# Seven block products in place of eight in the second layer's gated feed-forward of a two-layer hybrid backbone

## The chip, the cores and the metric

One NeuronCore of one Trainium2 chip runs the whole program. The metric is the device time of one execution in microseconds. The profile is of one execution; its span runs from the first instruction to the last.

## What is computed

Two layers, each a mixing sub-layer (three groups of heads) and a gated feed-forward. There are 512 latent and 256 context tokens; in layer 1's feed-forward only the 512 latent ones are left. The part that matters here:

```python
def rms_norm(x, g):
    xf = x.astype(F32)
    y = xf * lax.rsqrt(jnp.mean(xf * xf, axis=-1, keepdims=True) + EPS)
    return (y * g.astype(F32)).astype(x.dtype)

def conv_ffn(h, P):
    gt = dwconv(h @ P["w_gate"], P["ffn_conv_w"], P["ffn_conv_b"])
    return (jax.nn.silu(gt) * (h @ P["w_val"])) @ P["w_down"]
...
        h2 = modulate(rms_norm(x_lat, norm2_g[l]), sh2, sc2)
        x_lat = x_lat + g2 * conv_ffn(h2, P)
```

Here h is 512 x 1024, w_gate and w_val are 1024 x 2816, w_down is 2816 x 1024, and the convolution runs over three neighbouring tokens. All is float32.

## The kernel before

Activations lie transposed in SBUF, features on the 128 partitions and tokens along the free dimension: xT and the normed input have 8 blocks k of 128 features. Each float32 operand is split in a rounded part and a rest of a shorter format (hi and lo), and each product is made of three matmuls, hi x hi, hi x lo and lo x hi (mm3, L315 to L317). Weights are loaded as raw (L252, one DMA of 512 KB on SP's queue, three buffers), cast to whi by ScalarE (L260), and VectorE makes wlo = raw - whi (sub_lo, L108). The weight is the stationary operand, the tokens are the moving one.

The feed-forward runs over 22 tiles j of 128 hidden features, in two halves of 11. In a tile, TensorE makes the gate's and the value's product (pp, 8 blocks k each, 512 columns in layer 1); ScalarE makes the first tap with the bias (L1061), VectorE the two others (L1062, L1064), ScalarE the Silu (L99), VectorE the product with the value (L1069), and ft is split into gh (ScalarE, L1070) and gl (VectorE). After 11 tiles the down projection (pd, four pairs of 128 output features) adds into xT (L1100); the gate and value tiles have eight PSUM banks, shared with pd.

The input of layer 1's feed-forward is made by Norm.apply: for each k and each 256 tokens VectorE makes nt (L351), ScalarE hhi (L355) and VectorE hlo (L356); nt has three buffers. The first tile's matmuls follow k by k, and then ScalarE loads the table for Silu.

While layer 0's feed-forward runs, VectorE also makes layer 1's modulation by dot products (L232, in the first half) and splits layer 1's input weights ahead (split_ahead, L283 to L297: loads araw, writes both parts to DRAM). A scheduler orders the instructions on each engine by priorities; each engine then works strictly in that order. SP's queue issues all DMAs in order.

Of the kernel before, what the change touches and what calls it, by code (L numbers as in the profile page):

```python
# [16 lines left out]
P = 128  # L17
# [44 lines left out]
N1H, N1P = 5, 2  # L62

# [7 lines left out]
LPOS = (5, 2)  # L71

# [6 lines left out]
def tile_backbone(  # L79
# [27 lines left out]
    def sub_lo(o, a, hi, eng=None):  # L107
        (eng or V).tensor_sub(o, a, hi.bitcast(F32))  # L108
# [193 lines left out]

    def wsplit_of(key, src, shape, eng, tags=("hi", "lo"), p=None, **kw):
# [19 lines left out]
    class Norm:  # L323
        def __init__(self, np_, nb=2):
            self.p, self.nb = np_, nb
            self.ss = np_.tile([P, TOK], F32, tag="nss", name="nss", bufs=1)
            self.rs = np_.tile([P, TOK], F32, tag="nrs", name="nrs", bufs=1)
            self.begun = set()
# [19 lines left out]
        def apply(self, l, n, g, k, hhi, hlo):  # L348
# [5 lines left out]
            sh = modv[:, l, s, 3 * n, k:k + 1]  # L354
            r = S.activation(hhi[:, k, a:b], t[:, :b - a], AF.Identity, bias=sh)  # L355
# [16 lines left out]
    for l in range(DEPTH):  # L372
# [398 lines left out]
        yp = pool(ystack, f"y{l}", side)  # L771
# [182 lines left out]
        kvs.close()  # L954
# [9 lines left out]
        norm = Norm(np_)  # L964
        table(T_LNEXP)
        with ExitStack() as ph:
# [27 lines left out]
            for k in range(KD):  # L994
                norm.apply(l, 1, g0, k, hhi, hlo)
        if not last:
            ystack.close()
            layer.close()


        with ExitStack() as ph:
            hp = pool(ph, f"g_{l}", "right")
            sp = pool(ph, f"s4_{l}", "right")
# [12 lines left out]

            if not last:
                dots = ExitStack()
                dp = pool(dots, "dots", "left")
            HJ = NJ // 2  # L1020

            if not last:
                norm = Norm(np_)
            for half in range(2):
                gh = hp.tile([P, HJ, toks], F32R, tag="gh", name="gh", bufs=1)
                gl = hp.tile([P, HJ, toks], F32R, tag="gl", name="gl", bufs=1)
                for jj in range(HJ):
                    j = half * HJ + jj
                    pp = [[ps.tile([P, 512], F32, tag="acc", name="pp", bufs=8) for g in range(2)]
                          for s in range(nseg)]  # L1030
                    w = [wsplit(w_gv[l, j, g], [KD, P], "dve") for g in range(2)]

                    def gv(g, seg):
                        a, b, s = seg
                        o = pp[s][g][:, a - SEG[s][0]:b - SEG[s][0]]
                        for k in range(KD):
                            mm3(o, w[g][0][:, k], w[g][1][:, k], hhi[:, k, a:b], hlo[:, k, a:b], k == 0, k == KD - 1)

                    if j == 0:
# [16 lines left out]
                    t = sp.tile([P, TOK], F32, tag="ft", name="ft", bufs=FTB)
                    for s in range(nseg):
                        a, b = SEG[s]
                        gp = pp[s][0]
                        n = b - a  # L1060
                        S.activation(t[:, a:b], gp[:, :n], AF.Identity, bias=fb[:, l, j:j + 1], scale=fw[:, l, j, 1:2])  # L1061
                        V.scalar_tensor_tensor(out=t[:, a + 1:b], in0=gp[:, 0:n - 1], scalar=fw[:, l, j, 0:1],  # L1062
                                               in1=t[:, a + 1:b], op0=ALU.mult, op1=ALU.add)
                        V.scalar_tensor_tensor(out=t[:, a:b - 1], in0=gp[:, 1:n], scalar=fw[:, l, j, 2:3],  # L1064
                                               in1=t[:, a:b - 1], op0=ALU.mult, op1=ALU.add)
                    act(t[:, :toks], t[:, :toks], AF.Silu)
                    for s in range(nseg):
                        a, b = SEG[s]
                        V.tensor_mul(t[:, a:b], t[:, a:b], pp[s][1][:, :b - a])  # L1069
# [137 lines left out]
```

## Time and profile before

| | |
|---|---|
| median of 3 runs | 1595.66 us (1593.68 to 1596.8) |
| profiled execution | 1593.64 us |
| its span | 1591.9 us |
| TensorE busy | 1555.6 us, 98% of the span |
| VectorE busy | 1015.4 us, 64% |
| ScalarE busy | 643.0 us, 40% |
| GpSimd busy | 108.0 us, 7% |
| mean granted TensorE clock | 0.995 of full speed |
| layer 0, feed-forward | about 403 to 960 us |
| layer 1, feed-forward | about 1215 to 1588 us |

The shares are means over stages with different limits. The rows below give them by stage, then single instructions of the places that the change touches. A busy time of TensorE is modelled at its end, so starts are compared.

### The profile page before, as it was taken

Reading aid. Unit: us, or ns where it says so; the run is one execution under the profiler, and the core shown is the slowest. Engines: PE = TensorE matmul, PEld = TensorE weight load, DVE = VectorE, ACT = ScalarE, POOL = GpSimd, SP = SyncE. Lnnn points to the kernel's source line nnn. Section 1 sums busy time; section 2 is a strip of 40 time slices with the busy share of each in tenths; the row PEclk is TensorE's granted clock in tenths of the full one; section 3 lists DMA queues with packets and bytes.
Section 4 is the critical chain, followed back from the end, with each engine's and each line's share of the span. In section 5 each row is a group of like instructions: output and inputs, shape, how many; then the busy total and the mean of one; then the engine's idle time right before and its main releaser. Section 6 shows DMA issues by size and latency. Waiting matters only on the chain.

```text
span 1591.9 us, 21110 instructions
## 1 busy us (share of the span) xinstructions
PE 1555.6 (98%) x8186; PEld 1287.7 (81%) x8186; DVE 1015.4 (64%) x1713; ACT 643.0 (40%) x1115; POOL 108.0 (7%) x128
## 2 busy tenths in 40 slices
PE   6999998999999999999999999999999999999999
PEld 4767786778888888888888887877778888888888
DVE  4489879969999972244454454996977444334433
ACT  5423668853522221133333333265765333133321
POOL 1102134310000000000000000002410000000000
PEclk8999999999999999999999999999999999999999
DMA  8652110014355872126666486542011222322232
GB/s 286 240 187 63 54 54 14 14 67 172 106 185 190 291 246 63 64 68 220 196 199 210 147 278 220 195 153 81 14 54 57 99 97 86 99 94 93 93 110 89
DMA packets 76372, 208.77 MB, mean 131 GB/s; under 512 B 11504, under 2 KB 13808, under 8 KB 76144
## 3 DMA queue, kind: packets, MB, share of 16 engines
q1 hardware_dynamic: 76272, 207.43, 39.5%
q8 instruction: 64, 1.05, 0.3%
q14 instruction: 36, 0.29, 0.1%
HBM read 183.28 MB, written 24.12 MB: 130 GB/s over the span
## 4 chain that ended last, share of the span: by engine, by line
PE 75%; DVE 2%; ACT 1%; issue 0%; POOLq 0%; DVEq 0%; ACTq 0%
PE pp L316 13%; PE pp L315 13%; PE pp L317 13%; PE pd L315 6%; PE pd L317 6%; PE pd L316 6%; PE acc L483 2%; PE acc L484 2%; PE acc L491 2%; PE wo L315 2%; PE wo L316 2%; PE wo L317 2%; PE po L902 1%; PE accC L540 0%; PE accC L538 0%; PE accC L539 0%
## 5 line engine op out<-in xcount | busy, mean ns | idle before, releaser
L260 ACT CAST whi<-raw 128x1024 fp32r<-128x1024 f32 (+1 forms) x174 | 178.2, 1026 | 521.0 <-PE pp L316 247.8
L316 PE MATMUL pp<-hlo,whi 128*128 128x512 f32 (+1 forms) x1072 | 380.6, 356 | 0.8 <-DVE hlo L356 0.8
L315 PE MATMUL pp<-hhi,whi 128*128 128x512 f32 (+1 forms) x1072 | 379.9, 356 | 1.5 <-ACT whi L260 1.3
L317 PE MATMUL pp<-hhi,wlo 128*128 128x512 f32 (+1 forms) x1072 | 378.9, 354 | 0.0
L108 DVE TENSOR_TENSOR wlo<-raw,whi 128x1024 fp32r<-128x1024 f32 (+2 forms) x159 | 189.4, 1194 | 284.4 <-ACT whi L260 279.5
L315 PEld LDWEIGHTS pp<-hhi,whi 128*128 128x128 f32 x1072 | 201.4, 188 | 35.2 <-ACT whi L260 2.7
L316 PEld LDWEIGHTS pp<-hlo,whi 128*128 128x128 f32 x1072 | 201.5, 188 | 32.7 <-DVE hlo L356 1.5
L317 PEld LDWEIGHTS pp<-hhi,wlo 128*128 128x128 f32 x1072 | 201.5, 188 | 31.3
L315 PE MATMUL pd<-gh,whi 128*128 128x512 f32 (+1 forms) x550 | 192.9, 351 | 0.0
L316 PE MATMUL pd<-gl,whi 128*128 128x512 f32 (+1 forms) x550 | 192.3, 350 | 0.0
L317 PE MATMUL pd<-gh,wlo 128*128 128x512 f32 (+1 forms) x550 | 192.3, 350 | 0.0
L317 PEld LDWEIGHTS pd<-gh,wlo 128*128 128x128 f32 x550 | 103.4, 188 | 15.2
L316 PEld LDWEIGHTS pd<-gl,whi 128*128 128x128 f32 x550 | 103.5, 188 | 15.0
L315 PEld LDWEIGHTS pd<-gh,whi 128*128 128x128 f32 x550 | 103.4, 188 | 15.1
L733 DVE SCALAR_TENSOR_TENSOR cacc<-cin,cw,cacc 128x783 f32<-128x783 f32 (+1 forms) x120 | 105.0, 927 | 3.4 <-ACT cacc L728 3.4
L1069 DVE TENSOR_TENSOR ft<-ft,pp 128x256 f32<-128x256 f32 (+1 forms) x66 | 39.4, 598 | 96.2 <-PE pp L317 84.8
L232 DVE CUSTOM_DVE_ANT_0 mraw<-mraw,csil,bmod 128x1024 f32<-128x1024 f32 x64 | 81.6, 1278 | 7.5 <-DMA mraw<-in_w_modT_dram 7.3
L483 PE MATMUL acc<-whi,hhi 128*128 128x512 f32 x192 | 78.5, 409 | 0.0
L99 ACT ACTIVATE ft<-ft 128x768 f32<-128x768 f32 (+1 forms) x44 | 32.5, 740 | 113.0 <-DVE ft L1064 112.9
L484 PE MATMUL acc<-whi,hlo 128*128 128x512 f32 x192 | 76.6, 399 | 0.0
L99 ACT ACTIVATE e<-pss,mx 128x768 f32<-128x768 f32 (+1 forms) x80 | 65.1, 816 | 16.3 <-DVE mx L857 14.8
L857 DVE TENSOR_REDUCE mx<-pss 128x1 f32<-128x768 f32 (+1 forms) x80 | 67.2, 845 | 4.1 <-PE pss L855 3.1
(220 smaller groups left out, 2498.3 us busy)
## 6 DMA issues: line engine op xcount, KB each, us to landing
raw<-in_w_gv_dram SPq DMA_DIRECT2D x88, 512.0 KB, 3.3
mraw<-in_w_modT_dram SPq DMA_DIRECT2D x64, 512.0 KB, 4.2
raw<-in_w_down_dram SPq DMA_DIRECT2D x34, 512.0 KB, 3.6
wh<-in SPq DMA_DIRECT2D x24, 512.0 KB, 4.4
wl<-in SPq DMA_DIRECT2D x24, 512.0 KB, 4.3
raw<-in_w_in_dram SPq DMA_DIRECT2D x20, 512.0 KB, 3.7
araw<-in_w_in_dram SPq DMA_DIRECT2D x40, 256.0 KB, 3.4
in<-ahi SPq DMA_DIRECT2D x40, 256.0 KB, 4.6
```

The lines of the kernel that those rows point to most:

```text
L99: r = S.activation(out, in_, func, **kw)
L108: (eng or V).tensor_sub(o, a, hi.bitcast(F32))
L232: r = V.tensor_tensor_reduce(out=junk, in0=w, in1=csil[:, s], scale=1.0, scalar=bmod[:, l, i, f:f + 1], op0=ALU.mult, op1=ALU.add, accum_o ...
L260: S.copy(hi, raw)
L315: T.matmul(o, lhi, rhi, start=start, stop=False)
L316: T.matmul(o, lhi, rlo, start=False, stop=False)
L317: T.matmul(o, llo, rhi, start=False, stop=stop)
L483: T.matmul(pt[t], hhi[hs], wh[:, a], start=k2 + a == 0, stop=False)
L484: T.matmul(pt[t], hlo[hs], wh[:, a], start=False, stop=False)
L733: V.scalar_tensor_tensor(out=cacc[:, c, :cn], in0=cin[:, c, j:j + cn], scalar=cw[:, l, c, j:j + 1], in1=cacc[:, c, :cn], op0=ALU.mult, op1 ...
L857: V.tensor_reduce(out=mx, in_=pss[:, :nk * P], op=ALU.max, axis=AX.X, negate=True)
L1069: V.tensor_mul(t[:, a:b], t[:, a:b], pp[s][1][:, :b - a])
```

## The change

In layer 1's feed-forward, tiles 4 to 21 make gate and value together with seven block products in place of eight. The tokens are taken in blocks of 128: even blocks and odd blocks are the two columns of a 2 x 2 block product, the lower and the upper four k are its inner halves, gate and value are its rows. The eight products of a plain tile have each 4 blocks k and 256 columns; the seven need sums of the operands. Sums of the weights are made by sum_quarters (four VectorE operations of 512 columns a tile). For 14 tiles it runs in layer 0 (sum_ahead: two loads pgv, the sums, two writes to DRAM, all DMAs on SP's queue); for tiles 8, 9, 16 and 17 it runs in layer 1. Sums of the tokens are made once: GpSimd writes the full normed input hf from nt (a new instruction in Norm.apply), half_forms makes four sums, three of them split again in hi and lo, and third_form puts the fourth over the odd blocks of the lower half of hhi and hlo after the last plain tile.

A seven tile loads four weights (a1, two sums, a22: 1.75 MB). Its products go into three PSUM banks, al, de and be, in the order 1, 7 of the tile before, 5, 2, 4 of the tile before, 6, 3; al is read out after products 1 and 6 while later products add onto it. Read-outs go to gs and vs in SBUF by three ScalarE copies (L1232, L1234, L1238) and three VectorE sums (L1236, L1240, L1242); the product with the value is two operations of 256 columns (L1248, L1249). The tiles go in groups of 8, 8 and 6, with a down projection after each; layer 0 keeps 11 and 11 and plain tiles. Other edits free and take pools in another order.

```diff
+GROUPS = ((11, 11), (8, 8, 6))
+SEVEN = (False, True)
+NPLAIN = 4
...
+SUMJ = (0, 2, 4, 6, 8, 10)
+MSUM, ESUM = ((1, 2, 3), (0,)), ((0, 1, 2, 3), (0,))
+AHEAD = (4, 5, 6, 7, 10, 11, 12, 13, 14, 15, 18, 19, 20, 21)
...
+    def sum_quarters(gr, vr):
+
+        lo_, hi_ = slice(0, KD // 2), slice(KD // 2, KD)
+        r = V.tensor_add(vr[:, hi_], vr[:, lo_], vr[:, hi_])
+        V.tensor_sub(vr[:, lo_], gr[:, lo_], vr[:, lo_])
+        V.tensor_sub(gr[:, lo_], vr[:, hi_], gr[:, lo_])
+        V.tensor_sub(gr[:, hi_], gr[:, hi_], gr[:, lo_])
+        return r
+
+    def sum_ahead(sp):
...
+            if ready:
+                x, w = ready
+                summed[x] = dram.tile([P, 2, KD, P], F32, name=f"gv_{x}")
+                r = sum_quarters(*w)
+                tc.add_manual_dep(r.ins, after.name, NOSYNC, reason="data of the step before")
+                for g in range(2):
+                    nc.sync.dma_start(out=summed[x][:, g], in_=w[g])
+            if j is not None:
+                w = [sp.tile([P, KD, P], F32, tag=t, name="pgv", bufs=2) for t in ("hi", "lo")]
+                for g in range(2):
+                    nc.sync.dma_start(out=w[g], in_=w_gv[1, j, g])
...
-        def apply(self, l, n, g, k, hhi, hlo):
+        def apply(self, l, n, g, k, hhi, hlo, full=None):
...
+            if full is not None:
+                G.tensor_scalar(out=full[:, k, a:b], in0=t[:, :b - a], scalar1=sh, scalar2=None, op0=ALU.add)
...
+        def half_forms(g):
...
+            V.tensor_sub(t1, q12, q11)
+            V.tensor_sub(t2, q22, t1)
+            V.tensor_sub(t3, q22, q12)
+            V.tensor_sub(t4, q21, t2)
+            for x, (fh, fl) in ((1, f1), (2, f2), (4, f4)):
+                S.copy(fh[:, :, a // 2:b // 2], tt[x])
+                sub_lo(fl[:, :, a // 2:b // 2], tt[x], fh[:, :, a // 2:b // 2])
+
+        def third_form():
+
+            for g, t3 in t3s.items():
...
+                o = od(hhi, slice(0, KD // 2), a, b)
+                S.copy(o, t3)
+                sub_lo(od(hlo, slice(0, KD // 2), a, b), t3, o)
...
+            def seven_weights(j):
+                a1 = wload(w_gv[l, j, 0], [KD, P])
+                ws = {}
+                for g, p in ((1, wp), (0, rg)):
+                    ws[g] = p.tile([P, KD, P], F32, tag="raw", name="raw", bufs=RAWB if p is wp else 2)
+                    nc.sync.dma_start(out=ws[g], in_=summed[j][:, g] if j in summed else w_gv[l, j, g])
+                a22 = rg.tile([P, KH2, P], F32, tag="a22", name="a22", bufs=2)
+                nc.sync.dma_start(out=a22, in_=w_gv[l, j, 1, :, KH2:])
...
+                return {1: (a1, 0), 2: (a1, 1), 7: (sv, 0), 5: (sv, 1), 6: (sg, 0), 3: (sg, 1), 4: ((h2, l2), None)}
...
+                    prod(j, i, {1: al, 6: al, 7: al, 4: al, 5: de, 3: de, 2: be}[i], i in (1, 5, 2))
+                    with tc.high_priority(offset=EVP):
+                        if i == 1:
+                            S.copy(evt(gs), blk(al))
+                        elif i == 5:
+                            S.copy(vs, de)
+                        elif i == 2:
+                            V.tensor_add(evt(gs), blk(be), evt(gs))
+                        elif i == 6:
+                            S.copy(odt(gs), blk(al))
+                        elif i == 3:
+                            V.tensor_add(odt(gs), blk(de), odt(gs))
+                        elif i == 7:
+                            V.tensor_add(vs, al, vs)
+
+                def end(j, gh, gl, jj):
...
+                    t = taps(j, lambda s: gs[:, SEG[s][0]:SEG[s][1]])
+                    V.tensor_mul(evt(t), evt(t), blk(al))
+                    V.tensor_mul(odt(t), odt(t), blk(vs))
+                    finish(t, gh, gl, jj)
...
-            HJ = NJ // 2
...
-            for half in range(2):
...
+            for half, HJ in enumerate(HJS):
+                jb = sum(HJS[:half])
...
+                    for n, j in enumerate(js + [None]):
+                        prev = js[n - 1] if n else None
+                        if half == 0 and n == 1:
+                            third_form()
+                        for i, of in ((1, j), (7, prev), (5, j), (2, j), (4, prev), (6, j), (3, j)):
+                            if of is not None:
+                                step(of, i)
+                                if i == 4:
+                                    end(of, gh, gl, of - jb)
```

VectorE before, one plain tile of layer 1 (gl here is of the tile before; ft, pp and wlo as above):

```order
L108 TENSOR_TENSOR gl<-ft,gh 128x512
L108 TENSOR_TENSOR wlo<-raw,whi 128x1024
L1062 SCALAR_TENSOR_TENSOR ft<-pp,fw,ft 128x511
L1064 SCALAR_TENSOR_TENSOR ft<-pp,fw,ft 128x511
L1069 TENSOR_TENSOR ft<-ft,pp 128x512
L108 TENSOR_TENSOR wlo<-raw,whi 128x1024
L108 TENSOR_TENSOR gl<-ft,gh 128x512
```

VectorE now, one seven tile in the steady state, from product 3's read-out (a_ is the raw a22; sv is a PSUM bank):

```order
L1240 TENSOR_TENSOR gs<-sv,gs 128x2x128
L1143 SCALAR_TENSOR_TENSOR ft<-gs,fw,ft 128x511
L1145 SCALAR_TENSOR_TENSOR ft<-gs,fw,ft 128x511
L1242 TENSOR_TENSOR vs<-sv,vs 128x256
L119 TENSOR_TENSOR wlo<-raw,whi 128x1024
L1249 TENSOR_TENSOR ft<-ft,vs 128x2x128
L1236 TENSOR_TENSOR gs<-sv,gs 128x2x128
L119 TENSOR_TENSOR wlo<-raw,whi 128x1024
L119 TENSOR_TENSOR a22l<-a_13680,a22h 128x512
L1248 TENSOR_TENSOR ft<-ft,sv 128x2x128
L119 TENSOR_TENSOR gl<-ft,gh 128x512
```

Six rows a tile (the seventh above is the next gl) became twelve: the eleven here and a third wlo, whose place shifts by a row or two from tile to tile. The read-outs of the banks now stand between the weights' rows.

SP's queue before, in layer 0's second half (ahi and araw are the parts of layer 1's input weights written ahead; raw is the next tile's weight):

```order
L296 DMA in_0_7117<-ahi 128x512
L297 DMA in_0_7117<-araw 128x512
L283 DMA araw<-in_w_in_dram 128x512 x3
L252 DMA raw<-in_w_gv_dram 128x1024 x2
L296 DMA in_1_7258<-ahi 128x512
```

SP's queue now, at a like place:

```order
L307 DMA in_2_6612<-ahi 128x512
L308 DMA in_2_6612<-araw 128x512
L294 DMA araw<-in_w_in_dram 128x512 x2
L337 DMA gv_6629<-pgv 128x1024
L294 DMA araw<-in_w_in_dram 128x512
L337 DMA gv_6629<-pgv 128x1024
L341 DMA pgv<-in_w_gv_dram 128x1024
L263 DMA raw<-in_w_gv_dram 128x1024
L341 DMA pgv<-in_w_gv_dram 128x1024
L307 DMA in_3_6764<-ahi 128x512 x2
```

The writes of the sums (gv) and the next loads (pgv) stand between the writes of split_ahead and the raw loads of the following tiles.

VectorE before, at the end of Norm.apply in layer 1, with the first wlo of the next tile:

```order
L351 SCALAR_TENSOR_TENSOR nt_11118<-xT_61,amod_70,nrs_10709 128x256
L356 SCALAR_TENSOR_TENSOR hlo_10707<-nt_11114,modv_67,hhi_10706 128x256
L351 SCALAR_TENSOR_TENSOR nt_11122<-xT_61,amod_70,nrs_10709 128x256
L356 SCALAR_TENSOR_TENSOR hlo_10707<-nt_11118,modv_67,hhi_10706 128x256
L356 SCALAR_TENSOR_TENSOR hlo_10707<-nt_11122,modv_67,hhi_10706 128x256
L108 TENSOR_TENSOR wlo_11188<-raw_11185,whi_11187 128x1024
```

VectorE now at this place (nt_11308 is the last; GpSimd's 16 hf are the last work on its queue):

```order
L394 SCALAR_TENSOR_TENSOR nt_11308<-xT_61,amod_70,nrs_10862 128x256
L401 SCALAR_TENSOR_TENSOR hlo_10860<-nt_11303,modv_67,hhi_10859 128x256
L1075 TENSOR_TENSOR t1_11370<-hf_11164 128x512
L401 SCALAR_TENSOR_TENSOR hlo_10860<-nt_11308,modv_67,hhi_10859 128x256
L1076 TENSOR_TENSOR t2_11371<-hf_11164,t1_11370 128x512
L1077 TENSOR_TENSOR t3_0_11153<-hf_11164 128x512
L1078 TENSOR_TENSOR t4_11372<-hf_11164,t2_11371 128x512
L119 TENSOR_TENSOR wlo_11388<-raw_11385,whi_11387 128x1024
```

The sums t1 to t4 of half_forms moved between the last hlo and the wlo rows of the next tile, and each nt now takes a buffer that GpSimd's hf has to have read.

## Rows read from the trace of the kernel before

**Rows 1.** The stages: busy us of each engine, their instructions, granted clock, DMA share, GB/s.

```profile
588.00:682.00 94.00, 94.00 (x540) 81.98 (x539) 26.60 (x36) 13.13 (x14) 0.00 (x0) 1.00 0.25 77
682.00:867.00 185.00, 185.00 (x1050) 160.97 (x1049) 90.75 (x127) 70.26 (x96) 0.00 (x0) 1.00 0.56 175
867.00:960.00 93.00, 93.00 (x522) 80.47 (x522) 43.33 (x73) 29.04 (x50) 1.46 (x1) 1.00 0.66 217
...
1247.00:1342.00 95.00, 95.00 (x409) 76.48 (x408) 43.85 (x51) 34.24 (x44) 0.00 (x0) 1.00 0.28 93
```

**Rows 2.** The page: GB/s moved by DMA in 40 equal slices of the span.

```profile
GB/s 286 240 187 63 54 54 14 14 67 172 106 185 190 291 246 63 64 68 220 196 199 210 147 278 220 195 153 81 14 54 57 99 97 86 99 94 93 93 110 89
```

**Rows 3.** VectorE's timeline over one plain tile of layer 1 and into the next.

```profile
1292.38 1.22 DVE L108 TENSOR_TENSOR wlo<-raw,whi 128x1024 fp32r<-128x1024 f32 x1 [3.77 <-ACT whi L260]
...
1297.98 1.23 DVE L108 TENSOR_TENSOR wlo<-raw,whi 128x1024 fp32r<-128x1024 f32 x1
1299.13 0.68 DVE L108 TENSOR_TENSOR gl<-ft,gh 128x512 fp32r<-128x512 f32 x1
1303.58 1.22 DVE L108 TENSOR_TENSOR wlo<-raw,whi 128x1024 fp32r<-128x1024 f32 x1 [3.77 <-ACT whi L260]
```

**Rows 4.** TensorE's timeline in the last down projection: start us, duration us, engine, line, operation.

```profile
1575.94 0.28 PE L315 MATMUL pd<-gh,whi 128*128 128x256 f32 x1
...
1587.30 0.28 PE L315 MATMUL pd<-gh,whi 128*128 128x256 f32 x1
```

**Rows 5.** Weight loads under matmuls of 256 columns: timeline.

```profile
524.73 0.19 PEld L316 LDWEIGHTS pp<-hlo,whi 128*128 128x128 f32 x1
524.84 0.19 PEld L317 LDWEIGHTS pp<-hhi,wlo 128*128 128x128 f32 x1
```

**Rows 6.** Matmuls of 256 columns, moving operand in pieces: min, median, max ns.

```profile
L315 PE MATMUL pg<-vbh,whi x4: 280/290/290, 1026.1 to 1029.5; 128*128 128x256 f32 x4
```

**Rows 7.** VectorE's groups by shape from 1210 us on: busy us, mean ns, idle before them.

```profile
L1064 DVE SCALAR_TENSOR_TENSOR ft<-pp,fw,ft 128x511 f32<-128x511 f32 x22 | 16.5, 750 | 0.8
L338 DVE TENSOR_TENSOR nss<-nss,nsq 128x256 f32<-128x256 f32 x5 | 2.1, 421 | 1.1 <-ACT nsq L337 1.1
```

**Rows 8.** ScalarE's groups by shape from 1210 us on; its copies out of PSUM.

```profile
L260 ACT CAST whi<-raw 128x1024 fp32r<-128x1024 f32 x59 | 61.8, 1049 | 164.9 <-PE pp L316 103.1 <-PE pd L316 61.7
L1061 ACT ACTIVATE ft<-pp,fb,fw 128x512 f32<-128x512 f32 x22 | 17.1, 776 | 0.0
L1070 ACT CAST gh<-ft 128x512 fp32r<-128x512 f32 x22 | 13.7, 621 | 1.1 <-DVE ft L1069 1.1
...
L905 ACT COPY o<-po x20: 359/372/389, 249.2 to 1180.7; 128x256 f32<-128x256 f32 x20
```

**Rows 9.** Start of layer 1's feed-forward: timelines of VectorE, ScalarE, TensorE.

```profile
1212.04 0.48 DVE L351 SCALAR_TENSOR_TENSOR nt<-xT,amod,nrs 128x256 f32<-128x256 f32 x1 [0.39 <-ACT nrs L99]
...
1226.78 0.48 DVE L356 SCALAR_TENSOR_TENSOR hlo<-nt,modv,hhi 128x256 fp32r<-128x256 f32 x1 [0.18 <-ACT hhi L355]
...
1228.06 1.99 ACT L260 CAST whi<-raw 128x1024 fp32r<-128x1024 f32 x2
...
1229.15 0.50 PE L315 MATMUL pp<-hhi,whi 128*128 128x512 f32 x1 [1.06 <-ACT whi L260]
```

**Rows 10.** GpSimd beside VectorE in attention: tiles (min, median, max ns), timelines.

```profile
L874 POOL TENSOR_SCALAR dg<-epsi,sm x40: 446/448/1519, 242.0 to 1171.1; 128x128 f32<-128x128 f32 x40
...
L907 POOL TENSOR_TENSOR osq<-osq,dg x20: 722/737/1372, 250.1 to 1182.0; 128x256 f32<-128x256 f32 x20
...
1159.96 1.16 POOL L907 TENSOR_TENSOR osq<-osq,dg 128x256 f32<-128x256 f32 x1 [2.96 <-ACT osq L906]
1160.44 0.95 DVE L917 SCALAR_TENSOR_TENSOR o<-o,gsub,osq 128x256 f32<-128x256 f32 x1
...
1152.53 1.46 POOL L874 TENSOR_SCALAR dg<-epsi,sm 128x128 f32<-128x128 f32 x1 [2.12 <-ACT e L99]
1153.34 0.49 DVE L917 SCALAR_TENSOR_TENSOR o<-o,gsub,osq 128x256 f32<-128x256 f32 x1
```

More of the change, by code (lines that the diff above doesn't have):

```diff
@@ L62 @@
 N1H, N1P = 5, 2
+EVP = 600
 VEV = 2
@@ L993, in tile_backbone @@
                     wout(mp2, (1,), w, [g1], ps, "acc", 8, (i,))
[L994 to L998, printed above, removed]
+        ystack.close()
+        if last:
+            kvs.close()
+        layer.close()
+        hf = None
+        if seven:
+            ht = pool(fst, f"ht{l}", "right")
+            f1, f2, f4 = [[ht.tile([P, KD // 2, toks // 2], F32R, name=f"f{x}{t}") for t in "hl"] for x in (1, 2, 4)]
+            t3s = {g: ht.tile([P, KD // 2, P], F32, name=f"t3_{g[0]}") for g in ngs}
@@ new lines, in tile_backbone, with ev, od @@
+        hp = pool(fst, f"g_{l}", "right")
+        sp = pool(fst, f"s4_{l}", "right")
+        hfs = ExitStack()
+        if seven:
+            hfp = pool(hfs, f"hf{l}", "right")
+            hf = hfp.tile([P, KD, toks], F32, name="hf")
+        for k in range(KD):
+            norm.apply(l, 1, g0, k, hhi, hlo, hf)
+        def ev(x, ks, a=0, b=None):
+            return x[:, ks, a:b or toks].rearrange("p k (n two q) -> p k n two q", two=2, q=P)[:, :, :, 0]
+        def od(x, ks, a=0, b=None):
+            return x[:, ks, a:b or toks].rearrange("p k (n two q) -> p k n two q", two=2, q=P)[:, :, :, 1]
@@ L1055, in tile_backbone @@
                         start_dots(norm2.last)
[L1056 to L1069, printed above, removed]
-                    r = S.copy(gh[:, jj], t[:, :toks])
-                    sub_lo(gl[:, jj], t[:, :toks], gh[:, jj])
-                    if not last and half:
-                        ahead.send(r.ins)
+                    rs, rv = plain_end(j, pp, gh, gl, j - jb)
+                    if seven and j < len(ngs):
+                        half_forms(ngs[j])
@@ L1095, in tile_backbone @@
                                             gh[:, j0 + jj, a:b], gl[:, j0 + jj, a:b], st_, sp_)
+                            if not last and mp2 in MSUM[half] and ci == 1:
+                                sums.send(rv.ins)
                         for g in gs:
@@ L1109, in tile_backbone @@
                             ahead.send(r.ins)
+                        if not last and mp2 in ESUM[half] and not gi:
+                            sums.send(rv.ins)
                         if tail and not last:
```

213 lines of the change are left out of this document (160 added, 53 removed).

## The prediction

> **What bounds the kernel now.** I read the profile by stage first, since the shares of the page mix stages. In both feed-forward parts TensorE is busy in all of the time shown, VectorE in 28 to 49% of it and ScalarE in 14 to 38% [rows 1]. The reader is to see three things there. TensorE is full in layer 1's gate/value stretch (95.00 us of 95.00), so only fewer columns streamed can shorten it. VectorE (43.85) and ScalarE (34.24) have room, which is what an exchange of products for sums would use up. DMA moves 93 GB/s, with 290 seen elsewhere in the same run [rows 2]. The granted clock is 1.00 of full speed (the 2.4 GHz level) in all of these stretches, and nothing in the change leaves TensorE idle long, so I keep it at that level.
>
> Second, what one product costs. A plain tile of layer 1 is 2 x 8 x 3 = 48 matmuls of 512 columns. VectorE's rows give its time: the first wlo of a tile starts at 1292.38 and, one tile on, at 1303.58, so a tile is 11.20 us and a matmul 0.2333 [rows 3]. In the last down projection 96 matmuls of 256 columns, from 1575.94 to 1587.30, take 11.36: 0.1183 each [rows 4]. The weight of each takes 0.19 to load, but the next load begins 0.11 after it [rows 5]: two loads overlap, and the matmul sets the pace.
>
> **The products.** A tile of seven block products is 7 x 4 x 3 = 84 matmuls of 256 columns, 84 x 0.1183 = 9.94 us. That is 1.26 less, and 18 x 1.26 = **22.7 us** over the tiles. If the cost went strictly with columns (half of 0.2333 is 0.1167) it would be 9.80 and 25.2; I take the measured stretch, which had a new weight for each matmul too. Half of the moving operands are now pieces of 128 columns that lie 256 apart. The trace has the pg products with pieces of 64: 280 to 290 ns a row, as the 0.28 of the plain ones of 256 [rows 4, 6]. So nothing for that.
>
> Here a rule of the Trainium skill speaks against the change. First the rows: they show weight loads of 0.19 us every 0.12 us under matmuls of the whole array. The Trainium skill (page "TensorE: Matmul & The Clock Gate", section "The mechanism") says that a weight load overlaps matmuls in flight only where its row group differs. The trace doesn't bear that out; where loads could not overlap one another, the tile would be 84 x 0.19 = 16.0 us and the kernel 18 x 4.8 = 86 us slower. It stays as a rival with a small chance.
>
> **VectorE and ScalarE in a seven tile.** VectorE's twelve instructions are three wlo (1.15 from start to start), a22l and gl (0.68 each), two taps (0.75 each) and five operations of 256 columns (0.42, as nss, for one from SBUF; taken as 0.44) [rows 3, 7]: 3.4 + 1.4 + 1.5 + 2.2 = 8.5 us, of a tile of 9.94. Before it was 2 x 1.2 + 1.5 + 0.7 + 0.7 = 5.3 of 11.20. ScalarE has three whi (1.05), a22h 0.62, the first tap 0.78, gh 0.62, Silu as much, and three copies out of PSUM of 256 columns (0.37): 3.15 + 2.64 + 1.1 = 6.9, for 4.1 [rows 8]. Both fit, VectorE at 85%. Does it fit in order? I laid the rows of the order on a tile, with t = 0 at the end of product 3 and products 1.42 apart. On VectorE, gs (0.44), one wlo (1.15), the taps (1.5) behind ScalarE's first tap, and vs: the bank that product 4 overwrites is free at about 4.2, and is wanted at 5.68. The wlo of the next pair ends at about 5.45, and product 6 wants it at 7.10. The rest (0.44 + 0.44 + 1.15 + 0.68 + 0.44 + 0.68) ends with gl at about 10.3, 0.4 into the next tile, and doesn't add up, since 8.5 is under 9.94. So TensorE keeps a margin of about 1.5 us and stays the bound: 0 for this.
>
> **Loads.** A seven tile loads 0.5 + 0.5 + 0.5 + 0.25 = 1.75 MB, for 1.0: 176 GB/s, where the run shows 286 and 291 in a slice [rows 2]. They are issued as buffers come free, most of a tile ahead: 0.
>
> **Layer 0.** Fourteen tiles are summed there: 4 x 0.68 us on VectorE each, 38 us, and 2 MB of DMA each (two loads, two writes). VectorE is busy 26.60 of 94 us in the first down projection (6 tiles), 90.75 of 185 in the second half of gate/value (5) and 43.33 of 93 in the second down (3) [rows 1], so 16, 14 and 8 us more find room. DMA there goes from 77 to about 211, from 175 to 232 and from 217 to 285 GB/s; the last is at the peak of [rows 2] for as long as it lasts. On SP's queue a write waits for VectorE's sums, and behind it stand raw loads for the tiles to come. Those wait for VectorE's wlo anyway, and the sums stand directly ahead of it. Taken: 0; if the loads of the last part fall behind, 3 x 2.1 MB at 290 GB/s is 22 us of transfer against 93 us that are 0.66 full, so at most a microsecond or two.
>
> **Start of layer 1's feed-forward.** This is where I put the cost. For each of 16 k GpSimd now also makes hf from nt, and with three nt buffers VectorE's nt(k+3) waits for GpSimd's hf(k); behind that nt stand all later hlo, and TensorE takes them as they come. From 1212.04 to 1226.78 VectorE runs without a pause; then come the last hhi on ScalarE, the table's load, two casts (from 1228.06) and TensorE at 1229.15, which had stood idle for 1.06 [rows 9]. A delay of the last hhi passes through whole. GpSimd's row nearest in operation is dg of 128 columns, 0.446 alone; nearest in size osq of 256, 0.72 alone [rows 10]. But the two engines get in each other's way: at 1159.96 osq took 1.16 and VectorE's o, beside it, 0.95 where it takes 0.48 elsewhere. At 1152.53 it was GpSimd alone that paid (1.46 for 0.45) and the o beside it took 0.49 [rows 10]. So one hf costs VectorE 0 to 0.47 us, and the last nt depends on 13 of them: 0 to 6.1. If VectorE always wins, it stops later at its wait, for GpSimd's 0.45 to 0.72; so 0 is unlikely. Some of it hides beside the four xT updates from PSUM. I take 0.3 each, nearer to the row where VectorE paid, **4.0 us**. The four sums of half_forms stand ahead of the next wlo; that wlo had to wait for the cast at 1229.1 anyway, so 0.3.
>
> **Group changes.** The tiles go in groups of 8, 8 and 6, where two of 11 were, so one more down projection: 8 more xT updates (each as long as a tap) on a VectorE that is over half idle there [rows 1, 7]. The sums of tiles 8, 9, 16 and 17 lie there too, 5.4 us a time. The first products after a plain tile, or after a down projection, want three pairs at once, and third_form's copies can only start when tile 3's last matmul is done: 0.1 to 0.5 each at three places. Taken: **1.0 us**; bounds 0 and 3.
>
> Sum: 22.7 - 4.3 - 1.0 = 17.4. The profiled execution took 1593.64 (span 1591.9 and 1.74 around it), which gives 1576.2; the median of the runs is 1595.66, 2.0 above, which gives **1578**. With every bound at its best it is 1570.5 (25.2 and no cost), at its worst (start 6.4, changes 3) 1582.4.
>
> **Rivals.**
> - *hf stands in VectorE's way whole.* Each of the 13 costs the 0.72 of osq, not 0.3: 9.4 for 4.0, 1583.4. For it: at 1160.44 VectorE paid for two thirds of an instruction (0.47 of 0.72). Against it: at 1152.53 it paid nothing. The Trainium skill has this as a rule (page "SBUF — State Buffer", section "Who interferes with whom"): a VectorE instruction with two SBUF inputs and a GpSimd instruction that reads SBUF exclude each other, and the loser stands for the whole of the other; both instructions of the apply have two.
> - *VectorE's loop becomes the bound.* If the three places where it waits for ScalarE in order (first tap 0.78, Silu and gh 0.62 each) are not covered, a tile is 8.5 + 2.0 = 10.5: 18 x 0.70 = 12.6, less 5.3, gain 7: 1588. For it: 85% busy, and ScalarE's copies wait for the ends of products. Against it: before, each of these waits has a wlo or a tap of another tile to hide it, and the order keeps that.
> - *Slower: the two queues lock step.* ScalarE takes its work in order; a copy waiting for product 6 holds up gh and the next whi behind it, and VectorE's wlo, and then TensorE. If one whi (1.05) more is in the ring, a tile is 11.55, and with the start's 5.3 the kernel is 18 x 0.35 + 5.3 = 12 us slower: 1607. It decides from a tile of 11.20 - 5.3/18 = 10.9 us on. Against it: ScalarE has 3 us of room in a tile.
> - *Weight loads don't overlap* at a whole program's length: 86 us slower, 1682. Against it: the 96 in a row.
> - *hf costs nothing and the changes neither:* 1573. This lies within the forecast's own range.
>
> The change does what it says in the order: 84 rows of 256 columns in a tile, for 48 of 512.
>
> **How the numbers follow.** Forecast 0.62, own range 1571 to 1582.4; hf whole 0.13; VectorE's loop 0.13, 1585 to 1596; lock step 0.10; weight loads 0.02. For 8 in 10 the range takes the first two and some of the loop's: 1571 to 1590. A measurement of this kernel can tell 0.2%, 3.2 us, from no change. Faster: the first two and 0.09 of the loop, 0.84; same 0.04, the rest of the loop; slower 0.12, lock step and weight loads.
>
> **What would show it.** A stretch of seven tiles without idle TensorE, first wlo to first wlo 9.94 apart; VectorE there 85% busy. In the apply, hlo rows more than 0.79 us apart a k, GpSimd rows of 0.5 to 1.2, and TensorE's restart 3 to 5 us later against the first hhi. It would be wrong if TensorE showed idle time before products 4 or 6 (the loop), before product 1 (loads), or if matmuls of 256 columns stood over 0.12 apart.

## The result, and the profile after

The changed kernel takes 1575.41 us (median of 4 runs, 1574.56 to 1576.31), the kernel before 1595.93 in the same job: a ratio of 0.9874, 95% interval 0.9857 to 0.9891, so 20.5 us faster (17 to 23). The prediction was 1578, between 1571 and 1590. In a second job with other kernels it took 1575.22 beside 1594.18, ratio 0.9880 (0.9865 to 0.9895).

The page of the changed kernel: span, busy time of each engine, DMA by slice, and the new loads of layer 0 (KB each, us to landing).

```profile
span 1574.5 us, 22904 instructions
...
PE 1537.3 (98%) x8804; PEld 1305.1 (83%) x8804; DVE 1128.5 (72%) x1916; ACT 693.3 (44%) x1212; POOL 125.0 (8%) x144
...
GB/s 284 236 200 64 54 54 14 14 42 200 69 195 185 281 266 181 239 211 212 287 255 249 286 228 250 202 174 107 28 16 79 124 171 108 166 187 116 154 115 94
...
pgv<-in_w_gv_dram SPq DMA_DIRECT2D x28, 512.0 KB, 5.5
```

TensorE gave up 18 us of busy time and is still at 98%; VectorE went from 64% to 72% of the span. The reader should next look at the stages, as in [rows 1]. The first row lies in tiles 8 to 15, the others in layer 0.

```profile
core 0: us, PE busy (x) PEld busy (x) DVE busy (x) ACT busy (x) POOL busy (x), PEclk, DMA share, GB/s
1353.00:1430.00 77.00, 77.00 (x649) 77.00 (x648) 58.73 (x88) 48.18 (x75) 0.00 (x0) 1.00 0.52 169
...
588.00:682.00 94.00, 94.00 (x542) 82.11 (x541) 39.21 (x57) 13.02 (x14) 0.00 (x0) 1.00 0.59 206
682.00:867.00 185.00, 185.00 (x1048) 160.88 (x1048) 102.89 (x148) 69.84 (x97) 0.00 (x0) 1.00 0.72 245
867.00:944.00 77.00, 77.00 (x456) 67.81 (x455) 39.43 (x61) 21.20 (x35) 0.00 (x0) 1.00 0.78 261
```

TensorE is full in all four, at the same granted clock. VectorE is busy 58.73 of 77 us in the seven tiles, 76%; in layer 0 it took on 12 us in each of the first two stages, and DMA went from 77, 175 and 217 GB/s to 206, 245 and 261 (the last row ends at 944 us here, at 960 in [rows 1]). None of layer 0's stages grew: from its first pd matmul to its last it is 371.80 us before and now. VectorE's timeline shows a tile:

```profile
1370.48 1.23 DVE L119 TENSOR_TENSOR wlo<-raw,whi 128x1024 fp32r<-128x1024 f32 x1 [0.35 <-ACT whi L1174]
...
1373.07 0.42 DVE L1242 TENSOR_TENSOR vs<-sv,vs 128x256 f32<-128x256 f32 x1
1373.40 1.22 DVE L119 TENSOR_TENSOR wlo<-raw,whi 128x1024 fp32r<-128x1024 f32 x1
...
1380.52 1.23 DVE L119 TENSOR_TENSOR wlo<-raw,whi 128x1024 fp32r<-128x1024 f32 x1 [0.40 <-ACT whi L1174]
```

From one wlo to the same one a tile on it is 10.04 us; over a whole group the tiles are 10.00 apart (10.02 and 9.99 in turn), where 9.94 was forecast. What TensorE waited for from 1205 us on:

```profile
PE pp L358 <- ACT whi L271: 1.0, 2, 0.8
PE pp L359 <- DVE hlo L401: 0.2, 1, 0.2
...
```

So there is no wait in the seven tiles, and none at a change of groups. The only place where the kernel lost time is the start. Before, in timelines of TensorE and VectorE:

```profile
1215.08 0.29 PE L315 MATMUL pp<-hhi,whi 128*128 128x256 f32 x1
...
1224.93 0.48 DVE L351 SCALAR_TENSOR_TENSOR nt<-xT,amod,nrs 128x256 f32<-128x256 f32 x1
...
1225.73 0.47 DVE L351 SCALAR_TENSOR_TENSOR nt<-xT,amod,nrs 128x256 f32<-128x256 f32 x1
```

and now, in timelines of TensorE, VectorE, GpSimd, ScalarE and TensorE again:

```profile
1215.88 0.28 PE L358 MATMUL pp<-hhi,whi 128*128 128x256 f32 x1
...
1228.27 0.47 DVE L394 SCALAR_TENSOR_TENSOR nt<-xT,amod,nrs 128x256 f32<-128x256 f32 x1
1228.67 0.69 DVE L401 SCALAR_TENSOR_TENSOR hlo<-nt,modv,hhi 128x256 fp32r<-128x256 f32 x1
1229.29 0.47 DVE L394 SCALAR_TENSOR_TENSOR nt<-xT,amod,nrs 128x256 f32<-128x256 f32 x1
...
1230.30 0.68 DVE L1075 TENSOR_TENSOR t<-hf 128x512 f32<-128x512 f32 x1
1230.90 0.69 DVE L401 SCALAR_TENSOR_TENSOR hlo<-nt,modv,hhi 128x256 fp32r<-128x256 f32 x1
...
1218.06 13.71 POOL L399 TENSOR_SCALAR hf<-nt,modv 128x256 f32<-128x256 f32 x13 [0.48 <-DVE nt L394]
...
1230.32 1.28 ACT L104 ACT_TABLE_LOAD   x1
...
1231.65 0.39 PE L359 MATMUL pp<-hlo,whi 128*128 128x256 f32 x1 [0.25 <-DVE hlo L401]
...
1233.17 0.50 PE L358 MATMUL pp<-hhi,whi 128*128 128x512 f32 x1 [0.79 <-ACT whi L271]
```

From the first pp matmul of layer 1 (1215.88) to TensorE's restart behind the table load (1233.17) it is 17.29 us. Before it was 14.07: the first pp was at 1215.08 and the restart at 1229.15 [rows 9]. VectorE's pair of nt and hlo takes 1.01 us a k, for 0.79 before, and GpSimd's 13 hf in a row 13.71 us, 1.05 each. The 3.2 us have two parts. The last nt starts 13.41 us after the first pp (1229.29), for 10.65 before (1225.73): 2.8 us. Behind it t1 of half_forms (L1075, at 1230.30) stands ahead of the last hlo, and TensorE waits 0.25 us for that hlo; ScalarE's cast then starts 0.47 us after the end of the table load and not at once, so the other 0.5 us is VectorE's order.

### The profile page after: what moved, and what is told of

Same layout as the page of the kernel before. It is cut to its first block, busy times and chain, and to the rows that moved or that the text cites. A ratio compares the mean times of both kernels' runs of the same rounds, so it can differ in the third digit from the quotient of the medians.

```text
span 1574.5 us, 22904 instructions
## 1 busy us (share of the span) xinstructions
PE 1537.3 (98%) x8804; PEld 1305.1 (83%) x8804; DVE 1128.5 (72%) x1916; ACT 693.3 (44%) x1212; POOL 125.0 (8%) x144
## 4 chain that ended last, share of the span: by engine, by line
PE 74%; DVE 3%; ACT 1%; issue 0%; POOL 0%; DVEq 0%; ACTq 0%; POOLq 0%
PE pp L359 9%; PE pp L358 9%; PE pp L360 9%; PE pd L358 7%; PE pd L360 7%; PE pd L359 7%; PE sv L358 4%; PE sv L359 4%; PE sv L360 4%; PE acc L528 2%; PE acc L536 2%; PE acc L529 2%; PE wo L358 2%; PE wo L359 2%; PE wo L360 2%; PE po L947 1%
## 5 line engine op out<-in xcount | busy, mean ns | idle before, releaser
L359 PE MATMUL pp<-hlo,whi 128*128 128x256 f32 (+1 forms) x784 | 267.0, 342 | 1.5 <-DVE hlo L401 1.1
L358 PE MATMUL pp<-hhi,whi 128*128 128x256 f32 (+1 forms) x784 | 266.1, 341 | 1.3 <-ACT whi L271 1.0
L360 PE MATMUL pp<-hhi,wlo 128*128 128x256 f32 (+1 forms) x784 | 265.0, 339 | 0.0
L359 PEld LDWEIGHTS pp<-hlo,whi 128*128 128x128 f32 x784 | 147.4, 188 | 22.8 <-DVE hlo L401 4.8
L358 PEld LDWEIGHTS pp<-hhi,whi 128*128 128x128 f32 x784 | 147.3, 188 | 22.0 <-ACT whi L271 2.5
L360 PEld LDWEIGHTS pp<-hhi,wlo 128*128 128x128 f32 x784 | 147.4, 188 | 18.2 <-DVE wlo L119 0.2
L359 PE MATMUL sv<-hlo,whi 128*128 128x256 f32 x288 | 81.2, 282 | 0.0
L358 PE MATMUL sv<-hhi,whi 128*128 128x256 f32 x288 | 81.1, 282 | 0.0
L360 PE MATMUL sv<-hhi,wlo 128*128 128x256 f32 x288 | 81.1, 282 | 0.0
L1174 ACT CAST whi<-raw 128x1024 fp32r<-128x1024 f32 x54 | 56.5, 1050 | 51.2 <-PE sv L359 32.8
```

The lines of the kernel that those rows point to most:

```text
L358: T.matmul(o, lhi, rhi, start=start, stop=False, skip_group_check=again)
L359: T.matmul(o, lhi, rlo, start=False, stop=False, skip_group_check=again)
L360: T.matmul(o, llo, rhi, start=False, stop=stop, skip_group_check=again)
L1174: S.copy(hi, src)
```

## The experiments

Two measures serve below. Medians and ratios are against the kernel before in the same job. The other is free of what happens earlier in a run: the time from the first pp matmul of layer 1 to the start of VectorE's last xT updates. It is 373.13 us before (1215.08 to 1588.21), 354.89 in the changed kernel and 354.90 in its second profile.

**hf made by VectorE, not by GpSimd.**

```diff
-            norm.apply(l, 1, g0, k, hhi, hlo, hf)
+            norm.apply(l, 1, g0, k, hhi, hlo)
...
+            for ks in (lo_, hi_):
+                V.tensor_add(hf[:, ks, a:b], hhi[:, ks, a:b].bitcast(F32), hlo[:, ks, a:b].bitcast(F32))
```

> GpSimd makes no hf; VectorE makes it as hhi + hlo in half_forms (two additions of 128x1024 for each of the two token segments, about 4.6 us during tiles 0 to 3). The theory that GpSimd beside VectorE is what delays the start of layer 1's feed-forward: VectorE's nt and hlo come back to 0.79 us a k from 1.01, TensorE restarts about 3.3 us earlier against its first pp, and the kernel stands 3 us under the changed one, at about 1572. The rival that the start is late for the sums of half_forms ahead of the next wlo, or for the scheduler's other order there: restart as late as in the changed kernel, 1575 to 1577.

Measured: 1573.63 us, ratio 0.9873 (0.9858 to 0.9888); 352.54 us by the second measure, 2.35 under the changed kernel. TensorE, VectorE and TensorE at the start:

```profile
1214.23 0.28 PE L358 MATMUL pp<-hhi,whi 128*128 128x256 f32 x1
...
1224.37 0.48 DVE L394 SCALAR_TENSOR_TENSOR nt<-xT,amod,nrs 128x256 f32<-128x256 f32 x1
1224.76 0.48 DVE L401 SCALAR_TENSOR_TENSOR hlo<-nt,modv,hhi 128x256 fp32r<-128x256 f32 x1
1225.16 0.48 DVE L394 SCALAR_TENSOR_TENSOR nt<-xT,amod,nrs 128x256 f32<-128x256 f32 x1
...
1225.95 1.22 DVE L1073 TENSOR_TENSOR hf<-hhi,hlo 128x1024 f32<-128x1024 f32 x1
1227.09 0.48 DVE L401 SCALAR_TENSOR_TENSOR hlo<-nt,modv,hhi 128x256 fp32r<-128x256 f32 x1
...
1227.62 0.39 PE L359 MATMUL pp<-hlo,whi 128*128 128x256 f32 x1 [0.56 <-DVE hlo L401]
...
1229.14 0.50 PE L358 MATMUL pp<-hhi,whi 128*128 128x512 f32 x1 [0.78 <-ACT whi L271]
```

With GpSimd silent, hlo is back at 0.48 and a pair at 0.79. The restart comes 14.91 us after the first pp. The additional VectorE work (4.6 us) cost nothing but its place: the first addition, at 1225.95, stands ahead of the last hlo, and TensorE waits 0.56 for that. So GpSimd beside VectorE caused most of the late start; of its 3.2 us this run gives back 2.4, and most of the rest is an instruction of half_forms ahead of the last hlo, here as in the changed kernel. The medians of two jobs are too coarse to show it (0.9873 against 0.9874).

**Six nt buffers, GpSimd still making hf.** The changed kernel has three.

```diff
-            t = self.p.tile([P, 512], F32, tag="nnt", name="nt", bufs=NTB)
+            t = self.p.tile([P, 512], F32, tag="nnt", name="nt", bufs=6 if (l, n) == (1, 1) else NTB)
```

> Six nt buffers in place of three in this norm, GpSimd still making hf. The prediction's mechanism had two parts: VectorE's nt(k+3) waits for hf(k), and the two engines lengthen each other. If the wait for buffers sets the pace, VectorE comes back to 0.79 us a k and the restart moves 2 to 3 us towards the first pp (17.3 after it in the changed kernel). If only the lengthening does, hlo stays at 0.69 beside hf, 1.01 a k, restart 17.0 to 17.5.

Measured: one run of 1578.55 us; the granted clock stood at 0.5 for 3.4 us behind its restart, and the second measure is 356.47. TensorE's first pp, VectorE's pairs, TensorE's restart:

```profile
1216.55 0.28 PE L358 MATMUL pp<-hhi,whi 128*128 128x256 f32 x1
...
1227.31 0.69 DVE L401 SCALAR_TENSOR_TENSOR hlo<-nt,modv,hhi 128x256 fp32r<-128x256 f32 x1
...
1228.32 0.69 DVE L401 SCALAR_TENSOR_TENSOR hlo<-nt,modv,hhi 128x256 fp32r<-128x256 f32 x1
...
1233.85 0.50 PE L358 MATMUL pp<-hhi,whi 128*128 128x512 f32 x1 [0.78 <-ACT whi L271]
```

hlo stays at 0.69, a pair at 1.01, the restart 17.30 us after the first pp. The wait for buffers was no part of the cost; VectorE's instructions are lengthened beside GpSimd's.

**All tiles plain, sums still made in layer 0.**

```diff
-SEVEN = (False, True)
+SEVEN = (False, False)
```

> All 22 tiles of layer 1 are plain, in groups of 8, 8 and 6; the weights' sums are still made and written in layer 0, and nothing reads them; no hf. The theory that the sums in layer 0, their DMAs and the third down projection cost nothing, and that the products of seven carry the whole gain: as the kernel before, 1596 within 2 us, layer 0's four stages as long as before within 0.2 us each. The rival that the layout of groups and pools brings some of the gain by itself: 1590 to 1593. The rival that the sums cost and hide a larger gain: 1598 or more.

Measured: 1593.70 us beside 1594.27, ratio 0.9998 (0.9989 to 1.0007). The second measure is 373.31 for 373.13. Layer 0's stages:

```profile
588.00:682.00 94.00, 94.00 (x540) 82.05 (x539) 39.76 (x56) 13.13 (x14) 0.00 (x0) 1.00 0.59 209
682.00:867.00 185.00, 185.00 (x1049) 160.96 (x1048) 102.85 (x148) 70.27 (x96) 0.00 (x0) 1.00 0.72 244
867.00:960.00 93.00, 93.00 (x524) 80.68 (x524) 51.29 (x86) 29.16 (x50) 1.46 (x1) 1.00 0.77 261
```

From layer 0's first pd to its last it is 371.79 us, for 371.80 before. The sums, with 29 MB more of DMA, the third down projection and the new pools cost and bring nothing that the interval (under 2 us) or the second measure shows. The gain lies in the products.

**No sums ahead.**

```diff
-AHEAD = (4, 5, 6, 7, 10, 11, 12, 13, 14, 15, 18, 19, 20, 21)
+AHEAD = ()
```

> No sums in layer 0: all 18 seven tiles make them in layer 1, with four more VectorE operations of 512 columns (2.4 us) a tile. VectorE's 7.6 us of a tile become 10.0 of 10.00, with waits over it. The theory that VectorE's loop then sets the pace: tiles of 10.7 to 11.5 us instead of 10.00, idle TensorE before products, 1586 to 1600. The rival that the loop has room enough, also through the down projections: 1575 to 1578.

Measured: 1576.49 us, ratio 0.9884 (0.9871 to 0.9898). My theory fell. Stage of the seven tiles, as above:

```profile
1353.00:1430.00 77.00, 77.00 (x649) 77.00 (x648) 70.82 (x112) 47.98 (x75) 0.00 (x0) 1.00 0.49 170
```

VectorE is now busy 70.82 of 77 us, 92%, and the tiles are still 10.00 apart. By the second measure the run is 1.3 us over the changed kernel: TensorE's granted clock was at 0.5 in tile 1 for some microseconds, which cost 1.6 (more on this below), and the restart came 0.3 earlier. So VectorE has room for the sums in layer 1, and the part of the change that makes them in layer 0 and keeps them in DRAM isn't needed.

**More work for VectorE in each seven tile.** Eight operations more, then twelve:

```diff
                             V.tensor_add(evt(gs), blk(be), evt(gs))
+                            for _ in range(8):
+                                V.tensor_tensor(out=evt(gs), in0=evt(gs), in1=evt(gs), op=ALU.max)
```

> Eight more VectorE operations of 256 columns (a maximum of gs with itself, about 0.35 us each, 2.8 us) in each seven tile behind L1236. The theory that VectorE is busy 7.6 of 10.00 us and has about 2 us to give: 10.4 of work a tile binds, tiles of 10.5 to 11.2, 1584 to 1597. The rival that waits on ScalarE leave it less room than the shares say: over 11.2 a tile, over 1597.

Measured: one run of 1576.41 us, the tiles 10.00 apart. The same stage:

```profile
1353.00:1430.00 77.00, 77.00 (x650) 77.00 (x649) 74.12 (x143) 46.56 (x73) 0.00 (x0) 1.00 0.50 170
```

VectorE is busy 96% of the time and TensorE never waits; the longer tiles that I expected didn't come. This isn't quite a steady state. An added operation takes 0.335 us from start to start, so eight make a tile's work 7.6 + 2.7 = 10.3 us, and VectorE falls behind: in the group of eight tiles its last product of a tile (ft<-ft,vs) comes up to 11 us later than in the changed kernel (up to 8 in the run without sums ahead), and is back within 4 us of it (at the same time) by the group's end. A longer group wasn't run. Then twelve:

> Twelve more VectorE operations of 256 columns in each seven tile, 4.1 us, on 7.6 busy. With eight the tile stayed 10.00 with VectorE busy at 96%. The theory that VectorE is bound by its work alone and not by waits in order: 11.5 to 11.8 a tile, 18 x 1.6 = 29 us slower than the changed kernel, about 1604. The rival that the waits on ScalarE come on top once it is full: 12.5 or more a tile, over 1618.

Measured: one run of 1590.49 us. Stage and TensorE's waits in the seven tiles:

```profile
1355.00:1430.00 75.00, 69.40 (x550) 67.33 (x550) 71.97 (x149) 38.86 (x58) 0.00 (x0) 0.98 0.46 147
...
PE sv L360 <- DVE wlo L119: 8.0, 3, 2.7
```

Now TensorE stands for VectorE's wlo. The three groups, with 4, 8 and 6 tiles, take 10.1, 11.3 and 10.8 us a tile, 10.9 in the mean: less than the 11.5 I expected, since part of the added work slides into the down projections (VectorE's busy time from 1312 to 1354 us went from 22.45 to 26.75 us). In part it is also the clock, which fell to 0.5 for 3.4 us behind the wait of 2.7 us. The work is now 7.6 + 4.0 = 11.6 us a tile. So in the seven tiles TensorE waits only where VectorE's work is well over the tile's time, and in no run for VectorE's order or its waits on ScalarE alone.

**rg on the other side of SBUF.** The pool rg holds half of the pairs of weights and all of a22.

```diff
-                        rg = pool(ph, f"rg{l}", "right")
+                        rg = pool(ph, f"rg{l}", "left")
```

> The pool rg, which holds half of the pairs of weights and all of a22, lies on the other side of SBUF; nothing else differs. In the changed kernel a product whose weights lie in rg takes 1.427 to 1.443 us and one whose weights lie in wp 1.413 to 1.419. The theory that the place of the weights in SBUF sets it: the products' times change, towards 1.42 each and 9.94 a tile. The rival that the place doesn't matter and something else of these products does (their banks, the moving forms): the same 10.00 a tile, the same pattern.

Measured: one run of 1575.33 us, beside a median of 1575.22 for the changed kernel; its tiles are 9.94 apart in all three groups. The first matmul of product 5 in two tiles after one another, in the changed kernel:

```profile
1362.18 0.28 PE L358 MATMUL sv<-f1h,whi 128*128 128x256 f32 x1
...
1372.19 0.28 PE L358 MATMUL sv<-f1h,whi 128*128 128x256 f32 x1
```

and with rg on the left:

```profile
1361.91 0.28 PE L358 MATMUL sv<-f1h,whi 128*128 128x256 f32 x1
...
1371.85 0.28 PE L358 MATMUL sv<-f1h,whi 128*128 128x256 f32 x1
```

10.01 and 9.94 us. In the changed kernel product 4, whose weights always lie in rg, took 1.440 to 1.443 us, and product 5 1.414 or 1.427 in turn, as its pair lay in wp or rg; with rg moved all products take 1.416 to 1.424. So the weights' place in SBUF sets it, and it is worth 0.06 x 18 = 1.1 us. Why one side is slower wasn't found out.

**Forms later, and one more seven tile.** On top of hf made by VectorE, half_forms after tiles 1 and 2:

```diff
-                    if seven and j < len(ngs):
-                        half_forms(ngs[j])
+                    if seven and 0 < j <= len(ngs):
+                        half_forms(ngs[j - 1])
```

> As the run with hf made by VectorE from hhi + hlo, and half_forms of the two segments after tiles 1 and 2 instead of 0 and 1. The theory that what is left of the late start there (TensorE's 0.56 us before the last hlo, which stands behind the additions) is VectorE's order: the last hlo directly behind its nt, TensorE's restart 14.1 to 14.4 us after the first pp as in the kernel before (17.3 in the changed one, 14.9 with hf later): 0.5 us under that run, about 3 under the changed one. The rival that the forms then come too late for the first seven tile: idle TensorE before its first products, as slow as the changed one or slower.

Measured: 1574.32 us, ratio 0.9871 (0.9855 to 0.9888). TensorE at the start, and a stretch behind its restart (busy us of the engines, then the granted clock):

```profile
1229.41 0.39 PE L359 MATMUL pp<-hlo,whi 128*128 128x256 f32 x1 [0.56 <-DVE hlo L401]
1230.93 0.50 PE L358 MATMUL pp<-hhi,whi 128*128 128x512 f32 x1 [0.78 <-ACT whi L271]
...
1232.20:1235.00 2.80, 2.80 (x8) 2.13 (x7) 2.80 (x5) 1.15 (x3) 0.00 (x0) 0.50 0.59 193
```

The wait of 0.56 is still there: the scheduler put an addition ahead of the last hlo in this version too, so the edit didn't do what it was to do. And the clock stood at 0.5 (its 1.2 GHz level) for some 3 us behind the restart, where the changed kernel's row for 1233.20 to 1236.00 has 1.00. Matmuls of 512 columns were 0.43 apart there, for 0.23. What TensorE had done before was alike in both: short waits in the apply, 0.56 or 0.25, then 0.78. Three plain tiles on top of these edits:

```diff
-NPLAIN = 4
+NPLAIN = 3
```

> The same with three plain tiles, 19 of seven products; tile 3's sums are made in layer 1. The theory that each further tile is worth 11.20 - 10.00 = 1.2 us: 1.2 under the run with four plain tiles. The rival that VectorE has no time for all forms and three pairs of weights by then: idle TensorE before tile 3's products, same or slower.

Measured: 1580.99 us, ratio 0.9915 (0.9900 to 0.9929); the rival was right. TensorE's waits before tile 3's products, and that stretch:

```profile
PE sv L358 <- ACT whi L1176: 2.4, 2, 1.9
PE sv L360 <- DVE wlo L119: 1.1, 1, 1.1
...
1252.00:1270.00 18.00, 14.52 (x93) 13.66 (x92) 14.05 (x19) 10.24 (x16) 0.00 (x0) 0.81 0.55 189
```

TensorE stood 3.5 us for weights, and the clock fell behind that (0.81 in the mean of 18 us). A tile that would have saved 1.2 us cost 4.6 by the second measure (358.72 for 354.08). (The version with four holds about 1.6 us of its own dip.) VectorE's room is gone just there: from 1242 to 1261 us it has no pause over 0.2 us, with forms, sums and three pairs of weights together.

**Both edits that paid.** hf by VectorE, bound to come after the last hlo, and rg on the left:

```diff
+                r = V.tensor_add(hf[:, ks, a:b], hhi[:, ks, a:b].bitcast(F32), hlo[:, ks, a:b].bitcast(F32))
+                tc.add_manual_dep(r.ins, norm2.last.name, NOSYNC, reason="data of the step before")
...
-                        rg = pool(ph, f"rg{l}", "right")
+                        rg = pool(ph, f"rg{l}", "left")
```

> Two edits: hf made by VectorE from hhi + hlo, bound to come behind the last hlo, and rg on the other side of SBUF. The theory: the start comes back to the kernel before's (restart 14.1 to 14.4 us after the first pp, 17.3 in the changed one), tiles of 9.94 instead of 10.00: 3.0 + 1.1 = 4 us under the changed kernel, 1571, ratio 0.985 to 0.986. The rival that the time given back at the start is lost again behind it (forms late for the first seven tile, as with three plain tiles): 1574 to 1576.

Measured: 1572.41 us, ratio 0.9865 (0.9849 to 0.9882); 351.14 us by the second measure, 3.75 under the changed kernel. First pp and restart:

```profile
1214.16 0.28 PE L358 MATMUL pp<-hhi,whi 128*128 128x256 f32 x1
...
1228.53 0.50 PE L358 MATMUL pp<-hhi,whi 128*128 128x512 f32 x1 [1.06 <-ACT whi L271]
```

14.37 us, and behind the apply TensorE waits 1.06, as in [rows 9]. Then the same without sums in layer 0:

> The same without sums in layer 0; all 18 tiles make them in layer 1. The theory that VectorE has room for them there (busy about 10.0 of 10.00 us without a longer tile in the run without sums ahead): as the run with both edits, within 1.5 us, tiles of 9.94. The rival that at 9.94 a tile VectorE's loop with the sums no longer fits: tiles over 10.0, 2 us or more slower.

Measured: 1571.05 us, ratio 0.9855 (0.9841 to 0.9870), 351.02 by the second measure. It is the fastest version here, 23 us under the kernel before, and simpler than the change: no sums ahead, no tensors in DRAM. The difference from the run before it is within the intervals. Last, the changed kernel once more, in the job of the versions with forms later and with three plain tiles:

> The changed kernel as it is, beside the others of this job on one chip. If the time of the changed kernel is a sum of its parts in layer 1 (products 22.7, less 1.1 for matmuls of 0.119 instead of 0.118, less 3.2 at the start): 18 us under the kernel before in runs whose granted clock dips alike; by the first job's medians 20.5. If the profile's second dip near 245 us comes in every run of it, the gain stays near 18; if in some, the runs spread over about 2 us.

Measured: 1575.22 us, ratio 0.9880 (0.9865 to 0.9895), spread over 2.8 us. Its profile has the dip of the clock near 245 us, as the first one has; the profile of the kernel before has none there. But it lacks a shorter dip near 140 us that both of these have: its layer 0 ends (last pd) at 955.76 us, for 957.33 in the first profile and 955.60 before. So what the clock takes isn't the same in every execution of one kernel.

## Why the prediction was right

**Products: right, 1.1 us too high.** I took 22.7 us; with tiles of 10.00 it is 18 x 1.20 = 21.6. The step that missed is the choice of the stretch of 0.1183 us a matmul from [rows 4]: it holds for those weights' place, and here half of the weights lay elsewhere, at 0.119 to 0.120. With rg moved the stretch of [rows 4] is met exactly. The weight loads did overlap, as [rows 5] showed: the tile of 10.00 us leaves 0.119 us a matmul, and the rival of 86 us is refuted. So is, for these matmuls, the rule of the Trainium skill (page "TensorE: Matmul & The Clock Gate", section "The mechanism") that a weight load overlaps matmuls in flight only where its row group differs.

**VectorE and ScalarE in a tile: right, for a margin that I undersized.** I worked out 8.5 us for VectorE, and the profile has 58.73/77 x 10 = 7.6. But for wlo I had added up durations that overlap by about 0.08 us each. The ends I laid out were early enough by far: with 2.7 us more the tile didn't grow, so the loop and the lock step, which I gave 0.23 together, were not near. It failed only with 4.0 us more, where the work exceeds the tile's time.

**Loads and layer 0: right.** All stages of layer 0 kept their length with up to 261 GB/s, also in the run with all tiles plain. I didn't ask whether the sums had to be there; the room I found in the tile (1.4 us by my account) looked too small for 2.4. It was 2.4.

**Start: the cost was right in place and, by a third too high, in size (4.3 forecast, 3.2 measured), for half of the mechanism.** That VectorE is lengthened beside GpSimd's hf is shown: VectorE pays 0.22 a k, hlo at 0.69 for 0.48, within my 0 to 0.47 and near my 0.3; over 13 of them that is 2.8 for my 4.0. That nt waits for its buffer isn't so; six buffers changed nothing. GpSimd's hf took 1.05, where I had 0.45 to 0.72 from other operations; no run has it undisturbed, so what GpSimd paid isn't known. The sums of half_forms, for which I took 0.3, cost 0.5, and not where I put them: I had them only ahead of the next wlo, but the order has t1 ahead of the last hlo, for which TensorE and with it the cast wait. The rival by which VectorE stands for the whole of each hf (9.4 us) is refuted. The rule of the Trainium skill beside it (page "SBUF — State Buffer", section "Who interferes with whom"), that the loser stands for the whole of the other's instruction, isn't borne out either: there is contention between the two, but of 0.2 us for one of two VectorE instructions, and both went on side by side.

**Group changes: 1.0 forecast, next to none found.** 21.6 - 3.2 = 18.4, and the second measure gives 373.13 - 354.89 = 18.24, so 0.2 is left for them.

**The sum.** 17.4 was forecast, and the two profiled spans differ by just 17.4 (1591.9 to 1574.5). That is partly luck. My products were 1.1 too high and my costs 1.9, which cancel in part. Layer 1's feed-forward gave 18.24. The mixing part of layer 1 became 0.9 us shorter (from layer 0's last pd to the first pp, 258.55 for 259.48; the version with all tiles plain has it too, the one with six nt buffers has not; its cause wasn't looked for), and the profiled run lost 1.7 us to a dip of the clock near 245 us that the profile of before doesn't have. By medians it is 19.0 and 20.5 in two jobs, which agrees with 18.24 + 0.9 within the intervals.

## What to carry to other kernels

Where TensorE is at 98%, an exchange of a matmul for VectorE's work pays in full as long as VectorE's work stays under the tile's time: here VectorE could be busy 96% of it before TensorE noticed, in groups of at most eight tiles behind which it caught up, so add up the work first, and build the elaborate way of moving work elsewhere (sums ahead, DRAM) only when the simple one is shown not to fit. Work that is put on GpSimd "for free" beside a VectorE that sets the pace isn't free; a little more VectorE work a few microseconds later was. When a gain hangs on the pace of matmuls, look at their spacing again in the new place: the same matmuls can differ by 1% with the place of the weights.

## What the runs showed of the hardware

- The spacing of 256-column matmuls went from 0.1183 to between 0.118 and 0.120 us with the pool of the weights, product by product, and back when the pool lay on the other side of SBUF: 10.00 and 9.94 us a tile. 
- Two-input VectorE instructions of 256 columns beside GpSimd's tensor_scalar of the same size: every second one 0.69 for 0.48 us, GpSimd's 1.05 (not seen undisturbed), in a steady lock step of 1.01 us.
- After short waits of TensorE at the start of layer 1's feed-forward the granted clock fell to 0.5 for some 3 us in some profiles (no sums ahead, six nt buffers, forms later) and not in others with the same waits (the changed kernel's two); each time it cost about 1.6 us. With 3.5 us of waits before tile 3 it fell for longer, 6.8 us. Runs of one kernel that differ by 1.5 to 3 us may differ in this alone.
